# Which 39 of 128 expert blocks are computed ahead of the expert loop and stored

## The chip, the cores and the metric

The kernel runs on one core of a Trainium2 chip. The metric is the device time of one execution in microseconds (us), the median of several runs. Before the change it is 2943.44 us (three runs, 2942.09 to 2951.27).

Five engines matter. PE is the matrix engine (PEld are its weight loads), DVE the vector engine, ACT the activation engine, POOL issues the indirect gathers, and SP issues the plain DMAs. Each works through its own instructions in a fixed order and waits on semaphores for the others.

## The reference

One decoder layer over 1024 tokens of width 1024, all in float32. A mixing part (retention heads and differential attention heads, an output projection and a residual) comes first. Then follows a layer of product-key experts:

```python
q = (xb @ wq).reshape(t, PEER_HEADS, 2, PEER_DQ // 2)
s = jnp.einsum('thpd,hpkd->thpk', q, subkeys).astype(jnp.float32)
s_top, i_top = lax.top_k(s, K)
cand = (s_top[:, :, 0, :, None] + s_top[:, :, 1, None, :]).reshape(t, PEER_HEADS, K * K)
c_top, c_idx = lax.top_k(cand, K)
...
e = i1 * N_KEYS + i2
g = jax.nn.softmax(c_top, axis=-1)
ue = jnp.take(u, e, axis=0)
ve = jnp.take(v, e, axis=0)
act = jax.nn.gelu(jnp.einsum('thkd,td->thk', ue, xb).astype(jnp.float32), approximate=False)
return jnp.einsum('thk,thkd->td', (g * act).astype(xb.dtype), ve)
```

There are 8 heads, 16 ranks in each (`K`) and 128 x 128 = 16384 experts. Each expert is one row of `u` and one of `v`. A residual and a final norm follow.

## The kernel before

**Two ways through the experts.** Tokens lie in eight tiles of 128. Five of them (640 tokens, `TB`) are "dense": every expert is computed for all of them, and a weight matrix that is zero nearly everywhere (`g_d` in DRAM) selects. The other three are "sparse": for each of them 128 rows of `u` and 128 rows of `v` are gathered by indirect DMA (POOL, L860 and L867), 768 gathers of 512 KB in all, and each is worked into the result by one DVE instruction (L862 for `u`, L869 for `v`). Five buffers (`ug`) hold gathered rows.

**The dense experts.** The 16384 experts are 128 blocks of 128. For one block, `experts_in` (L711) loads a block of `u` (`uraw`, L704, 512 KB), splits it into a high part (ACT, L706) and a low part (DVE, L708), runs 48 matmuls into two PSUM banks `psH` (L720 to L722: two halves of 320 tokens, eight chunks, three products each) and writes the GELU of it (ACT, L723) into a tile `ga` of 128 x 640. `ga` has two buffers, which all the blocks use in turn.

**Stored blocks.** Some blocks are computed before the expert loop, in `spills` (L728), woven between the steps of the routing and of `dense_routes`, and their activations are stored in DRAM (`hs_d`, 320 KB each). There are `SPILL` = 39 of them, those of the list `early`.

**The expert loop.** It runs over 32 groups of `EG` = 4 blocks. One group does this:

- One DMA loads the group's weights from `g_d` into `gt` (L787, 1280 KB, in runs of 512 bytes). `gt` has a single buffer, so the load waits until the last use of the group before.
- For each of its four blocks: the activations come either from `experts_in`, or, for a block in `early`, by one DMA from `hs_d` into a tile of the same two buffers (L802, called `gl` in the profile). DVE multiplies them in place by the weights (L806), ACT and DVE split the product into high and low parts `wh` (L810) and `wl` (L812). The block of `v` (`vraw`, L814, 512 KB) is loaded and split likewise (`vh` L816, `vl` L818).
- Then 120 matmuls of 512 columns (L794 to L796): ten units (five tiles, two halves) by four blocks by three products. Four units stay in PSUM over the whole loop (`kp`), six go through two PSUM banks `psV` and are added into SBUF by DVE after each group (L830, called room, acc, accS, accc_intra and accab).

**What sets the order.** A planner orders each engine's instructions at build time: it runs the program on a model of the engines, and whenever an engine is free in the model it takes the instruction that is ready and stands earliest in the program text. The text has the dense loop first and the gathers after it, so the gathers fill the places that the dense work leaves free in the model. On the chip this order is fixed: an instruction that has to wait holds up everything behind it on its engine. Gathers can start before the loop at a pace set by hand (`PER`); from the first L806 on they are free.

Of the kernel before, what the change touches and what calls it, by code (L numbers as in the profile page):

```python
# [27 lines left out]
DC = D // P  # L28
# [4 lines left out]
NK = 128  # L33
# [13 lines left out]
EG = 4  # L47
# [3 lines left out]
KL = 1  # L51
BIGS = 4
ROUTE = 6
MIX = 3
ACTS = 1
AHEAD = 1
SPILL = 39
# [42 lines left out]
def layer_kernel(ctx, tc, x, wt, wn, wo, wq, sk, ut, u, v, gmix, gffn, gfin, gsub, dlam, consts, alb, out):  # L100
    nc = tc.nc
    V, A, PE, G, SY = nc.vector, nc.scalar, nc.tensor, nc.gpsimd, nc.sync
# [16 lines left out]
    one = cp.tile([P, 1, 1], U32, name="one")  # L119
# [11 lines left out]
        return r  # L131

    def front(m, pp, cst, g0, nt, dense, late):
        """Steps of the layer up to the routing for tiles g0..g0+nt, in the rooms m."""
        n = nt * P
        first, last = g0 == 0, g0 + nt == NT
        halves = [(0, n)] if n <= 512 else [(0, n // 2), (n // 2, n)]
# [8 lines left out]
            return m.big[0].tile(shape, dt, tag=m.big[1], bufs=m.big[2], name=name)  # L146

        def chunk(src, shape):
            """Weights [128, k, m] in their hi and lo parts."""
            raw = wp.tile(shape, F32, tag="raw", bufs=RAW, name="wraw")  # L150
            SY.dma_start(raw, src)
            hi = wp.tile(shape, F32R, tag="uh", bufs=2, name="whi")
            A.activation(hi, raw, AF.Copy)  # L153
            lo = wp.tile(shape, F32R, tag="ul", bufs=2, name="wlo")
            V.tensor_sub(lo, raw, hi.bitcast(F32))  # L155
            return hi, lo

        def mm(ps, a, b, start, stop):
            """Adds the product of operands a and b, each (hi, lo)."""
            PE.matmul(ps, a[0], b[0], start=start, stop=False)  # L160
            PE.matmul(ps, a[0], b[1], start=False, stop=False)  # L161
            PE.matmul(ps, a[1], b[0], start=False, stop=stop)
# [33 lines left out]
            yield  # L196

        def split_t(src_of, name):
            """Transposes natural [128 t, 1024] tiles into [128, DC, n] operands."""
            th = m.hp.tile([P, DC, n], F32R, tag="hTh", name=name + "h")  # L200
            tl = m.hp.tile([P, DC, n], F32R, tag="hTl", name=name + "l")
            for t in range(nt):
                src = src_of(t)
                srcs = src if isinstance(src, tuple) else (src[:, :512], src[:, 512:])
                for q in range(2):
                    ps = bankB("psX").rearrange("p (c t) -> p c t", c=4)
                    for c in range(4):
                        PE.transpose(ps[:, c], srcs[q][:, c * P:(c + 1) * P], ident)
                    dst = th[:, 4 * q:4 * q + 4, t * P:(t + 1) * P]
                    A.activation(dst, ps, AF.Copy)  # L210
                    V.tensor_sub(tl[:, 4 * q:4 * q + 4, t * P:(t + 1) * P], ps, dst.bitcast(F32))
                yield "turned"
            return th, tl

        # input norm
        gm = big([P, D], "gmix")
        SY.dma_start(gm, gmix.to_broadcast([P, D]))

# [10 lines left out]

        yield "normed"  # L230

        # natural projections: rv, dv, rg
        rv = m.vp.tile([P, nt, 512], F32, tag="rv", name="rv")

        def put_dv(t, ps):
# [160 lines left out]
                V.scalar_tensor_tensor(yd[:, t, sl], yd[:, t, sl], rd[:, t, h:h + 1], cst["gsub"],  # L396
                                       op0=ALU.mult, op1=ALU.mult)

        # output projection and residual
        mx = yield from split_t(lambda t: (rg[:, t], yd[:, t]), "m")  # L400
        x2 = [p.tile([P, nt, 512], F32, tag=tg, name="x2" + tg) for p, tg in ((m.vp, "rv"), (fp, "R"))]
        for hf in range(2):
# [68 lines left out]
            yield  # L471

    class Routed:
        """What the routing of a group leaves for later: key ranks and scores."""

        def __init__(self, rp, nt, tags):
            n = nt * PH * K
# [3 lines left out]
            self.ci = rp.tile([P, nt, PH, K], U32, tag=tags[1], name="late1")  # L481

    def decode(rp, late, t, eqs=("eq", 1), tmp=("tmp", 1), cs=("c2", 1)):
        """Key indices i1, i2 of tile t as [token, (head, rank)]."""

        tmps = rp.tile([P, 7, PH, K], U32, tag=tmp[0], bufs=tmp[1], name="tmps")
        row, col, sh, up = (tmps[:, i] for i in range(4))
        shf = tmps[:, 4].bitcast(F32)
        V.tensor_single_scalar(row, late.ci[:, t], 4, op=ALU.logical_shift_right)
        V.tensor_single_scalar(col, late.ci[:, t], K - 1, op=ALU.bitwise_and)  # L490
        V.tensor_scalar(shf, row, 1.0, -1.0, op0=ALU.max, op1=ALU.mult)
        V.tensor_scalar_add(sh, shf, 5.0)
        V.tensor_tensor(up, col, sh, op=ALU.logical_shift_right)
        V.tensor_tensor(row, one.to_broadcast([P, PH, K]), row, op=ALU.logical_shift_left)
        V.tensor_single_scalar(row, row, 1, op=ALU.logical_shift_right)
        c2 = rp.tile([P, 2, PH * K, 2], F16, tag=cs[0], bufs=cs[1], name="c2")

        def two(a):
            return a.rearrange("p h k -> p (h k)")[:, :, None].to_broadcast([P, PH * K, 2])
        V.tensor_tensor(c2[:, 0], two(row), two(up), op=ALU.add)  # L500
        V.tensor_tensor(up, up, sh, op=ALU.logical_shift_left)
        V.tensor_tensor(c2[:, 1], two(col), two(up), op=ALU.subtract)
        ij = []
        for p in range(2):
            eq = rp.tile([P, PH, K, K], F16, tag=eqs[0], bufs=eqs[1], name="eq")
            V.tensor_tensor(eq.rearrange("p h k (a b) -> p (h k) a b", b=2),
                            iok.rearrange("p (a b) -> p a b", b=2)[:, None].to_broadcast([P, PH * K, K // 2, 2]),
                            c2[:, p, :, None].to_broadcast([P, PH * K, K // 2, 2]), op=ALU.is_equal)
            V.tensor_tensor(eq, eq, late.tf[:, t, :, p, None, :].to_broadcast([P, PH, K, K]), op=ALU.mult)
            w = K // 2  # L510
            while w > 1:
                V.tensor_add(eq[:, :, :, :w], eq[:, :, :, :w], eq[:, :, :, w:2 * w])
                w //= 2
            iF = tmps[:, 5 + p].bitcast(F32)
            V.tensor_add(iF, eq[:, :, :, 0], eq[:, :, :, 1])
            ij.append(iF)
        return ij

    def gates_of(rp, late, nt, tag):
        """Softmax of the scores of tiles 0..nt, in their place."""  # L520
        cv = late.cv.rearrange("p t h k -> p (t h) k")
        mz = rp.tile([P, 2, nt * PH], F32, tag=tag[0], bufs=tag[1], name="mz")
        V.tensor_copy(mz[:, 0], cv[:, :, 0])
        V.tensor_sub(cv, cv, mz[:, 0, :, None].to_broadcast([P, nt * PH, K]))
        A.activation(cv, cv, AF.Exp)
        V.tensor_reduce(mz[:, 1], cv, axis=AX.X, op=ALU.add)
        V.reciprocal(mz[:, 1], mz[:, 1])
        V.tensor_mul(cv, cv, mz[:, 1, :, None].to_broadcast([P, nt * PH, K]))

    def sparse_routes(rp, late, g0, nt, *rooms):  # L530
        """Steps that leave expert indices and weights of the sparse tiles."""
        gates_of(rp, late, nt, rooms[0])
        for lt in range(nt):
            t = ST.index(g0 + lt)
            V.tensor_copy(gA[t].rearrange("p (h k) -> p h k", h=PH), late.cv[:, lt])
            i1, i2 = decode(rp, late, lt, *rooms)
            V.scalar_tensor_tensor(i1, i1, float(NK), i2, op0=ALU.mult, op1=ALU.add)
            V.tensor_copy(idxA[t].rearrange("p (h k) -> p h k", h=PH), i1)
            yield

    def dense_routes(rp, gp, pp, late):
        """Steps that put the weight matrices of the dense tiles into DRAM."""
        before = None
        gates_of(rp, late, ND, ("mz", 1))
        for t in range(ND):
# [17 lines left out]
        yield from build_g(gp, pp, *before)  # L563

    def build_g(gp, pp, r, lo, tb):
        """Weight matrices of one token tile: G[i2, i1, token] into DRAM."""
        for s in range(P // GC):
            st = gp.tile([P, NK, GC], F32, tag="st", bufs=2, name="st")
            for q in range(GC // 8):
# [78 lines left out]
        return es.enter_context(tc.tile_pool(name=name, bufs=1, reuse_waits="tile", **kw))  # L648

    def weave(a, b, na=1, nb=1):  # L650
        """Steps of a and b in turn, nb of b to na of a."""
        i = j = 0
        while a is not None or b is not None:
            if b is None or (a is not None and i * nb <= j * na):
                i += 1
                try:
                    yield next(a)
                except StopIteration:
                    a = None
            else:  # L660
                j += 1
                try:
                    yield next(b)
                except StopIteration:
                    b = None
# [5 lines left out]
        return next(i for i in reversed(ins) if i.engine == V.engine).name  # L671

    def gated(g, per):
        """Opens the way for per of the gathered experts after each step of g."""
        due = 0.0
        for y in g:
            due += per[y == "turned"]
            while due >= 1.0:
                gates.append(last_dve())
                due -= 1.0  # L680
            yield y
# [27 lines left out]
        return uh, ul  # L709

    def experts_in(ei, bank):  # L711
        """Activations of 128 experts for all dense tokens: [expert, token]."""
        uh, ul = load_u(ei)
        xh, xl = late.nx
        ga = wp.tile([P, TB], F32, tag="ga", bufs=2, name="ga")
# [7 lines left out]
            A.activation(ga[:, sl], ps, AF.Gelu)  # L723
        return ga

    early = [ei for ei in range(NK) if ei % EG < MIX][:SPILL]

    def spills(pf):  # L728
        for i, ei in enumerate(early):
# [46 lines left out]
        V.scalar_tensor_tensor(j, acc, r, gfb, op0=ALU.mult, op1=ALU.mult)  # L776
        SY.dma_start(out[t], j)

    # experts of the dense tiles
    acc = {}  # L780
    for i, un in enumerate(units[KEEP:]):
        acc[un] = room[i]
# [56 lines left out]
                V.tensor_copy(a[:, sl], acc[t, hf])  # L839
        finish(dp, a, DT[t], wp.tile([P, D], F32, tag="raw", bufs=RAW, name="fin"))  # L840

    # experts of the sparse tiles, gathered
    nth = 0

    def gate(ins):
# [63 lines left out]
```

## Time and profile before

| | |
|---|---|
| median of the runs | 2943.44 us |
| span of the profiled execution | 2961.6 us |
| PE busy | 2799.5 us, 95% |
| DVE busy | 2355.3 us, 80% |
| ACT busy | 1064.6 us, 36% |
| POOL busy | 1056.9 us, 36% |
| moved by DMA | 742.90 MB, mean 251 GB/s |

The profile is of one execution, whose span was 18.2 us (0.6%) over the median of the timed runs. The expert loop takes from about 1370 us to the end; the mixing and the routing lie before it. The busy share of PE is an average over stages with different limits, and its matmuls overlap in time, so that the step from one matmul's start to the next one's, not the duration, says how fast they run.

### The profile page before, as it was taken

The numbers are of one execution on the slowest core, as the hardware profiler recorded it, in microseconds if no ns is written. First come the engines' busy times: TensorE is split into PE (matmuls) and PEld (weight loads), VectorE is DVE, ScalarE is ACT, GpSimd is POOL, SyncE is SP. The second block draws the span as 40 slices with busy tenths as digits, with TensorE's granted clock in tenths as the row PEclk, the third lists the DMA queues.
The fourth block names the chain that finished last, engine by engine and source line by source line (L and its number), as shares of the span: only waits on it lengthen the run. The fifth ranks groups of instructions, "written<-read, shape, count | busy, mean of one in ns | idle before, by whom it ended". The sixth has DMA issues, their size and how long they took to land.

```text
span 2961.6 us, 43054 instructions
## 1 busy us (share of the span) xinstructions
PE 2799.5 (95%) x16043; PEld 2478.4 (84%) x16043; DVE 2355.3 (80%) x4522; ACT 1064.6 (36%) x1882; POOL 1056.9 (36%) x786
## 2 busy tenths in 40 slices
PE   7989989998889999999989999999999999999998
PEld 6868877776679999998777788899989989999987
DVE  3455888756769999985777888888889988888988
ACT  4553334433333248996212222222322222222222
POOL 0000003423330000001545444566566666665554
PEclk9989998876989999999999999999999999999999
DMA  5334236744662226667888888899999999999997
GB/s 166 108 121 140 94 118 206 247 150 152 241 239 89 85 97 226 242 240 285 305 293 305 308 301 312 318 330 334 344 337 336 341 341 335 341 338 321 344 339 264
DMA packets 293956, 742.90 MB, mean 251 GB/s; under 512 B 23529, under 2 KB 118761, under 8 KB 293746
## 3 DMA queue, kind: packets, MB, share of 16 engines
q0 software_dynamic: 112320, 405.06, 38.8%
q1 hardware_dynamic: 181426, 335.09, 33.0%
q8 instruction: 125, 2.05, 0.3%
q14 instruction: 85, 0.70, 0.1%
HBM read 670.92 MB, written 69.14 MB: 250 GB/s over the span
## 4 chain that ended last, share of the span: by engine, by line
PE 35%; issue 27%; DMA 11%; DVE 9%; POOL 4%; ACT 1%; POOLq 0%; DVEq 0%; ACTq 0%
DMA gt<-g_d 5%; PE psH L722 4%; PE psH L721 4%; PE psH L720 4%; POOL vg L867 3%; DMA vg<-in_v,idx 3%; PE psV L794 3%; PE psV L795 3%; PE psV L796 3%; DMA gl<-hs_d 2%; DVE sa L869 2%; PE kp L795 2%; PE kp L794 2%; PE kp L796 2%; DVE vl L818 1%
## 5 line engine op out<-in xcount | busy, mean ns | idle before, releaser
L867 POOL DMA_INDIRECT vg<-in_v,idx x384 | 528.5, 1376 | 923.0 <-DVE ug L862 521.5
L860 POOL DMA_INDIRECT ug<-in_u,idx x384 | 520.9, 1356 | 522.1 <-DVE ug L862 370.7
L869 DVE SCALAR_TENSOR_TENSOR sa<-vg,shs,sa 128x1024 f32<-128x1024 f32 x384 | 492.4, 1282 | 42.3 <-DMA vg<-in_v,idx 38.7
L862 DVE SCALAR_TENSOR_TENSOR ug<-ug,sx 128x1024 f32<-128x1024 f32 x384 | 461.2, 1222 | 62.6 <-DMA ug<-in_u,idx 61.9
L720 PE MATMUL psH<-nh,uh 128*128 128x320 f32 x1424 | 439.7, 309 | 0.1
L721 PE MATMUL psH<-nl,uh 128*128 128x320 f32 x1424 | 439.6, 309 | 0.0
L722 PE MATMUL psH<-nh,ul 128*128 128x320 f32 x1424 | 438.7, 309 | 0.8 <-DVE ul L708 0.8
L794 PE MATMUL psV<-vh,wh 128*128 128x512 f32 x768 | 306.8, 401 | 36.3 <-DVE acc L830 35.8
L795 PE MATMUL psV<-vl,wh 128*128 128x512 f32 x768 | 305.0, 398 | 0.0
L796 PE MATMUL psV<-vh,wl 128*128 128x512 f32 x768 | 297.4, 396 | 0.0
L720 PEld LDWEIGHTS psH<-nh,uh 128*128 128x128 f32 x1424 | 267.5, 188 | 6.4 <-ACT uh L706 0.9
L721 PEld LDWEIGHTS psH<-nl,uh 128*128 128x128 f32 x1424 | 267.3, 188 | 5.2
L722 PEld LDWEIGHTS psH<-nh,ul 128*128 128x128 f32 x1424 | 267.1, 188 | 4.4 <-DVE ul L708 1.6
L723 ACT ACTIVATE ga<-psH 128x320 f32<-128x320 f32 x178 | 74.6, 426 | 438.4 <-PE psH L722 396.4
L706 ACT ACTIVATE uh<-uraw 128x1024 fp32r<-128x1024 f32 x128 | 135.7, 1060 | 209.7 <-PE psH L721 120.3
L794 PEld LDWEIGHTS psV<-vh,wh 128*128 128x128 f32 x768 | 147.9, 193 | 68.7 <-DVE acc L830 38.6
L720 PE MATMUL psHs<-nh,uh 128*128 128x320 f32 x624 | 196.3, 316 | 9.1 <-ACT ga L723 8.9
L153 ACT ACTIVATE whi<-wraw 128x1024 fp32r<-128x1024 f32 x104 | 110.1, 1059 | 258.4 <-PE psT L161 141.4
L155 DVE TENSOR_TENSOR wlo<-wraw,whi 128x1024 fp32r<-128x1024 f32 x104 | 126.9, 1220 | 94.6 <-ACT whi L153 92.3
L795 PE MATMUL kp<-vl,wh 128*128 128x512 f32 x512 | 199.2, 392 | 0.4 <-DVE vl L818 0.4
L794 PE MATMUL kp<-vh,wh 128*128 128x512 f32 x512 | 193.2, 393 | 4.7 <-ACT wh L810 4.7
L708 DVE TENSOR_TENSOR ul<-uraw,uh 128x1024 fp32r<-128x1024 f32 x128 | 156.4, 1222 | 48.7 <-ACT uh L706 48.6
(242 smaller groups left out, 6271.0 us busy)
## 6 DMA issues: line engine op xcount, KB each, us to landing
uraw<-in_ut SPq DMA_DIRECT2D x128, 512.0 KB, 6.3
vraw<-in_v SPq DMA_DIRECT2D x128, 512.0 KB, 6.9
g_d<-st SPq DMA_DIRECT2D x80, 512.0 KB, 4.7
gt<-g_d SPq DMA_DIRECT2D x32, 1280.0 KB, 18.0
wraw<-in_wt SPq DMA_DIRECT2D x32, 512.0 KB, 3.7
wraw<-in_wq SPq DMA_DIRECT2D x32, 512.0 KB, 3.8
hs_d<-ga SPq DMA_DIRECT2D x39, 320.0 KB, 2.6
gl<-hs_d SPq DMA_DIRECT2D x39, 320.0 KB, 5.9
```

Of the source, the lines that this page charges most:

```text
L706: A.activation(uh, raw, AF.Copy)
L708: V.tensor_sub(ul, raw, uh.bitcast(F32))
L720: PE.matmul(ps, uh[:, dc], xh[:, dc, sl], start=(dc == 0), stop=False)
L721: PE.matmul(ps, uh[:, dc], xl[:, dc, sl], start=False, stop=False)
L722: PE.matmul(ps, ul[:, dc], xh[:, dc, sl], start=False, stop=(dc == DC - 1))
L794: PE.matmul(ps, Wh[e][:, sl], Vh[e][:, so], start=start, stop=False)
L795: PE.matmul(ps, Wh[e][:, sl], Vl[e][:, so], start=False, stop=False)
L796: PE.matmul(ps, Wl[e][:, sl], Vh[e][:, so], start=False, stop=stop)
L860: G.indirect_dma_start(out=ug, out_offset=None, in_=u, in_offset=bass.IndirectOffsetOnAxis(ap=idxA[t][:, k:k + 1], axis=0))
L862: gate(V.scalar_tensor_tensor(ug, ug, 1.0, xt, op0=ALU.mult, op1=ALU.mult, accum_out=hs[:, k:k + 1]))
L867: G.indirect_dma_start(out=vg, out_offset=None, in_=v, in_offset=bass.IndirectOffsetOnAxis(ap=idxA[t][:, k:k + 1], axis=0))
L869: gate(V.scalar_tensor_tensor(ac, vg, hs[:, k:k + 1], ac, op0=ALU.mult, op1=ALU.add))
```

## The change

The list of stored blocks changes. Before, with `MIX` = 3, it held the first three of each group of four for groups 0 to 12. Now it holds the first block of all 32 groups and, with `MIX` = 4, the second block of every fourth group (0, 4, ... 24). It is 39 blocks in both.

```diff
-MIX = 3
+MIX = 4
...
-    early = [ei for ei in range(NK) if ei % EG < MIX][:SPILL]
+    shared = list(range(0, NK, EG))
+    early = shared + [g * EG + 1 for g in range(0, NK // EG, MIX)][:SPILL - len(shared)]
```

So groups 0 to 12 computed one block in the loop and loaded three, and groups 13 to 31 computed four. Now 25 groups compute three and load one, and seven groups compute two and load two. The rest of the diff takes comments out.

## Rows read from the trace of the kernel before

**Rows 1.** Stretches: us, busy of each engine (instructions), PE clock, DMA share, GB/s.

```profile
1408.66:1838.34 429.68, 394.00 (x1847) 334.29 (x1846) 342.63 (x372) 96.04 (x126) 201.53 (x144) 0.96 0.88 302
1931.45:2874.20 942.75, 942.23 (x5300) 860.11 (x5299) 828.88 (x1004) 242.32 (x347) 587.29 (x424) 1.00 0.95 337
```

**Rows 2.** SP's timeline: gt loads that bound the two stretches (start, us).

```profile
1408.66 0.37 SPq L787 DMA_DIRECT2D gt<-g_d  x1
...
1838.38 0.38 SPq L787 DMA_DIRECT2D gt<-g_d  x1
...
1931.48 0.38 SPq L787 DMA_DIRECT2D gt<-g_d  x1
...
2874.25 0.38 SPq L787 DMA_DIRECT2D gt<-g_d  x1
```

**Rows 3.** PE's timeline near 2248 and 2264 us: starts of matmuls.

```profile
2248.02 0.31 PE L721 MATMUL psH<-nl,uh 128*128 128x320 f32 x1
...
2248.90 0.31 PE L721 MATMUL psH<-nl,uh 128*128 128x320 f32 x1
...
2264.15 0.39 PE L794 MATMUL psV<-vh,wh 128*128 128x512 f32 x1
...
2268.00 0.39 PE L796 MATMUL kp<-vh,wl 128*128 128x512 f32 x1
```

**Rows 4.** Waits of PE in the first stretch: total us, times, longest.

```profile
PE psV L794 <- DVE acc L830: 34.7, 9, 5.6
```

**Rows 5.** Waits of DVE in the first stretch.

```profile
DVE gl L806 <- DMA gt<-g_d: 56.3, 9, 9.9
DVE gl L806 <- DMA gl<-hs_d: 14.3, 4, 7.2
```

**Rows 6.** DVE's timeline in one group of the first stretch.

```profile
1607.63 0.82 DVE L806 TENSOR_TENSOR ga<-ga,gt 128x640 f32<-128x640 f32 x1
...
1616.33 1.29 DVE L830 TENSOR_TENSOR room<-psV,room 128x512 f32<-128x512 f32 x2 [1.06 <-PE psV L796]
1617.53 1.27 DVE L869 SCALAR_TENSOR_TENSOR sa<-vg,shs,sa 128x1024 f32<-128x1024 f32 x1
1625.03 0.83 DVE L806 TENSOR_TENSOR gl<-gl,gt 128x640 f32<-128x640 f32 x1 [6.22 <-DMA gt<-g_d]
...
1628.43 0.69 DVE L830 TENSOR_TENSOR acc<-psV,acc 128x512 f32<-128x512 f32 x1
```

**Rows 7.** PE's timeline in the same group.

```profile
1629.17 0.50 PE L794 MATMUL psV<-vh,wh 128*128 128x512 f32 x1 [1.47 <-DVE acc L830]
```

**Rows 8.** Issues of the gt load, first stretch, then second: count, KB each, us to landing.

```profile
gt<-g_d SPq DMA_DIRECT2D x11, 1280.0 KB, 17.5
...
gt<-g_d SPq DMA_DIRECT2D x17, 1280.0 KB, 19.0
```

**Rows 9.** DVE's timeline in one group of the second stretch.

```profile
2261.93 0.82 DVE L806 TENSOR_TENSOR ga<-ga,gt 128x640 f32<-128x640 f32 x1
...
2294.08 0.81 DVE L806 TENSOR_TENSOR ga<-ga,gt 128x640 f32<-128x640 f32 x1
```

**Rows 10.** The gt load over the first stretch: its landing, least, median and most.

```profile
DMA to landing us min/median/max: 13.6/17.7/19.1
```

**Rows 11.** POOL's timeline near the end: two gathers that follow each other.

```profile
2701.98 1.28 POOL L867 DMA_INDIRECT vg<-in_v,idx  x1 [0.65 <-DVE sa L869]
2703.91 1.86 POOL L867 DMA_INDIRECT vg<-in_v,idx  x1 [0.65 <-DVE sa L869]
```

**Rows 12.** DVE's gather work by line, first stretch, then second.

```profile
L869 DVE SCALAR_TENSOR_TENSOR sa<-vg,shs,sa 128x1024 f32<-128x1024 f32 x125 | 160.3, 1282 | 6.0 <-DMA vg<-in_v,idx 4.9
L862 DVE SCALAR_TENSOR_TENSOR ug<-ug,sx 128x1024 f32<-128x1024 f32 x18 | 21.8, 1223 | 0.0
...
L869 DVE SCALAR_TENSOR_TENSOR sa<-vg,shs,sa 128x1024 f32<-128x1024 f32 x221 | 283.4, 1282 | 31.7 <-DMA vg<-in_v,idx 29.6
L862 DVE SCALAR_TENSOR_TENSOR ug<-ug,sx 128x1024 f32<-128x1024 f32 x202 | 242.6, 1223 | 35.9 <-DMA ug<-in_u,idx 35.7
```

## The prediction, made before the changed kernel was run

> **What bounds the kernel now.** I read the page's slices first. PE is busy everywhere, but DMA and DVE are lower around 1400 to 1850 us than after it. That is the expert loop's first part, the 13 groups that compute one block and load three. So I read the loop in two stretches, cut at starts of the gt load, which comes once in a group.
>
> First stretch: from 1408.66 to 1838.38 us there are eleven groups of one computed block [rows 2], 39.07 us each. PE's clock was at 0.96 of full speed, DMA at 0.88 [rows 1]. Second stretch: from 1931.48 to 2874.25 us there are 17 groups of four computed blocks [rows 2], 55.46 us each. PE was busy for 942.23 of 942.75 us, at full clock [rows 1].
>
> What would PE need alone? Six steps of psH take from 2248.02 to 2248.90, 0.147 us each; 17 steps of 512-column matmuls take from 2264.15 to 2268.00, 0.2265 us each [rows 3]. A computed block has 48 of the first, 7.0 us, and a group has 120 of the second, 27.2 us. That makes 34.2, 41.3, 48.3 and 55.3 us for one to four computed blocks. The last agrees with the 55.46 measured: the second stretch is bound by PE. The groups of the first lose 39.07 - 34.2 = 4.9 us each.
>
> The waits say how. PE waited nine times, 34.7 us in all, to start an output matmul (psV) until DVE had added up the bank of PSUM before it [rows 4]. DVE had not done that because the instruction ahead of it in its order, the first multiplication by the weights of the next group (L806), waited for that group's gt or its stored block: 56.3 + 14.3 = 70.6 us [rows 5]. One group shows the chain. The last L806 of a group ends at 1608.45 and frees the single gt buffer; DVE does its next instructions up to 1618.80, waits 6.22 us for the load, multiplies at 1625.03, and adds at 1628.43 [rows 6]; PE, which stood 1.47 us for it, goes on at 1629.17 [rows 7]. So the load takes 17.5 us [rows 8], and DVE has put the multiplication behind some 10 us of work: the order was planned for a shorter load.
>
> In the second stretch nothing of the kind happens. The first block of a group is computed there, its activations come late, and its multiplication stands at 2294.08, 31.3 us after the last one of the group before (2262.75) [rows 9], where the load of 19.0 us [rows 8] has long landed.
>
> **The change part by part.** 39 blocks are computed ahead as before, in as many steps, so the time up to the loop costs nothing either way; only the addresses differ. In the loop the sums are the same too: 13 x 1 + 19 x 4 = 89 computed blocks before, 25 x 3 + 7 x 2 = 89 after. What moves are 26 blocks each way. A computed block in a group means a load of 512 KB on SP, a conversion each on ACT and DVE, 48 matmuls and two GELUs; a stored one means a load of 320 KB on SP. SP's order and the shared ga buffers move with them: a stored load waits until a buffer is free, with the vraw and uraw loads behind it.
>
> (a) Gain on PE. If PE sets the pace of every group, the loop takes 25 x 48.3 + 7 x 41.3 = 1497 us, against 13 x 39.07 + 19 x 55.46 = 1562 now: 65 us less. It is the most that the change can bring.
>
> (b) Cost on DVE. Every group now begins with a stored block. Its multiplication needs nothing but gt, as in the first stretch, so the planner can set it again as soon as its model has the load landed, ahead of the psV sums. The stall that 13 groups had then comes to 32. DVE's busy time was 342.63 / 11 = 31.1 us in a group of one computed block and 828.88 / 17 = 48.8 in one of four [rows 1]; in between, 5.9 us a block, I put 37.0 for two and 42.9 for three. The gathers are in it: (125 + 18) / 11 = 13.0 and (221 + 202) / 17 = 24.9 a group [rows 12], so 17.0 and 20.9; in a straight line their sum over the loop stays what it was.
>
> The stall is the size that decides. Its bounds are zero, as in the second stretch, and the longest one seen, 9.9 us [rows 5]. The mean of the first stretch is 70.6 / 11 = 6.4. The load takes longer with more traffic, 17.5 us at 302 GB/s and 19.0 at 337 [rows 1, 8]; the new groups, at about 316 GB/s (5.3 MB of loads and 21 gathers of 0.52 MB in 51 us), add 0.6. I take 7.0. DVE's other idle time in the first stretch is (429.7 - 342.6 - 70.6) / 11 = 1.5 us.
>
> A group of three then takes DVE 42.9 + 7.0 + 1.5 = 51.4 us and one of two 45.5, more than PE's 48.3 and 41.3. The same sum for one computed block gives 31.1 + 6.4 + 1.5 = 39.0, what was measured, so in a group with this stall DVE, not PE, has set the time. The loop takes 25 x 51.4 + 7 x 45.5 = 1604 us, 42 us more. What goes: the 4.9 us that PE lost in each of 13 groups; what is late next: PE loses 3.1 us in each of 25 and 4.2 in each of seven. Each microsecond of stall is worth 32 us. At 5.7 the change is worth nothing, and under 3.9 PE takes over in the groups of three.
>
> (c) The tail. PE and the gathers end together now; with gathers spread in a straight line nothing changes there. ACT is busy for 242.32 of 942.75 us where four blocks are computed [rows 1], so its two conversions hide in any group.
>
> The sum is +42 us on the profiled execution (span 2961.6, 18.2 over the median); on the median of 2943.4 it gives 2985 us.
>
> One rule of the Trainium skill speaks against this. The gt load takes 13.6 us at the least in the first stretch [rows 10]. The page "DMA: Bandwidth & Descriptors", section "Anatomy of one DMA", fits 2.0 us and the bytes over 436 GB/s for one transfer: 5.0 us for this load, an estimate, which DVE would never wait for. The trace does not agree: 17.5 to 19.0, with gathers on the same engines. By the page the sum would be that of (a) alone.
>
> **Rivals.**
>
> *No stall: the load hides.* The multiplication stands later in DVE's order, or the matmuls of two or three computed blocks give PE enough to do while DVE waits. For it: four-block groups have it at 31.3 us, and the planner has twice or three times as many psH matmuls to put before the waiting psV. Against it: those matmuls stand in a fixed order too, planned for a load that is early. The time is 2943 - 65 = 2878.
>
> *Half a stall.* DVE reaches the multiplication later, since it also waits for gathers in a denser order; at a stall of 4.5 us a group of three takes 48.9, one of two 43.0, the loop 1524: -38, 2905. For it: loads as short as 13.6 us [rows 10]. Against it: longer loads with more traffic.
>
> *Gathers left for the end, on top of the stall.* If the planner finds room for one gather less in a group than the straight line says, 32 remain after the loop. There they go at the pace of POOL, 2703.91 - 2701.98 = 1.93 us each [rows 11], while the loop saves 1.28 us of DVE for each [rows 12]: 32 x 0.65 = 21 us more, 3006. Two less make 3027. It decides from the first gather that starts after the last psV sum. For it: the stored multiplication comes earlier in every group and leaves DVE less open time. Against it: DVE's open time in the plan depends on blocks, whose sum stays.
>
> **How the numbers follow.** The forecast, a stall of about 7 us in every group, gets 0.53; no stall 0.22; half a stall 0.13; gathers left over 0.12. A measurement of this kernel can tell about 0.3%, 9 us, from no change. The forecast's own range goes with stalls from 5.7 to 8.5 us, 2943 to 3033; some 0.06 of its chance lies within 9 us. Half a stall gives 0.10 to faster and 0.03 to no change, leftover gathers 0.10 to slower and 0.01 to each of the others. That makes faster 0.22 + 0.10 + 0.01 = 0.33, same 0.06 + 0.03 + 0.01 = 0.10, slower 0.47 + 0.10 = 0.57. The range of 8 in 10 goes from 2882, which leaves half of the no-stall case out, to 3035.
>
> **What would show it.** In the profile after, DVE's waits at the first L806 of a group: some 200 us in all for gt and stored blocks over 32 groups, where 11 groups had 70.6. Groups of 51 us between gt loads, with PE waiting for DVE's sum in most of them. The forecast is wrong if gt loads come 48.3 us apart and PE waits nowhere, or if the first L806 of a group stands 20 us or more after the last of the group before without a wait; a string of gathers after the last psV sum would speak for the third rival.

## The result and the profile after

The changed kernel takes 3054.63 us (median of four runs, 3053.14 to 3074.22) against 2943.28 beside it: 111 us slower, a ratio of 1.0385 with an interval of 1.0353 to 1.0417. The forecast had the direction and the stall of DVE in every group, but not what the stall costs: it had 42 us, and 3054.63 lies above its range. The profiled execution had a span of 3052.6 us, 91.0 more than that of before.

The loop in stretches, with the columns of [rows 1]. The first goes from the second to the last gt load, 30 groups; the other is the end:

```profile
1412.80:2963.20 1550.40, 1456.66 (x7614) 1292.64 (x7613) 1244.23 (x1486) 361.82 (x504) 807.52 (x598) 0.97 0.86 307
2963.20:3052.60 89.40, 71.56 (x358) 61.87 (x356) 73.74 (x83) 20.18 (x34) 40.07 (x31) 0.92 0.75 258
```

Before, the same 30 groups took 2874.25 - 1408.66 = 1465.6 us [rows 2], so 84.8 of the 91 us are here. The end took nearly as long as before, 89.4 us against 87.3. PE's clock is at 0.97 over all of these 30 groups, where before it was at 0.96 in the first stretch alone [rows 1].

What PE and what DVE waited for in this stretch (total us, times, longest), PE first, then DVE:

```profile
PE psV L795 <- DVE acc L831: 87.4, 27, 5.5
```

```profile
DVE gl L807 <- DMA gt<-g_d: 160.9, 25, 8.5
...
DVE gl L807 <- DMA gl<-hs_d: 36.8, 5, 8.9
```

These answer to [rows 4] and [rows 5]. DVE's wait is 197.7 us over 30 groups, 6.6 each, where 11 groups had 6.4 each. PE waits 2.9 us a group for the sum behind it, where it had 34.7 / 11 = 3.2. So the wait has come to every group, as big as it was. The gt load lands after 17.7 us at the median here. The Trainium skill ("DMA: Bandwidth & Descriptors", "Anatomy of one DMA") fits its 2.0 us and bytes over 436 GB/s to DMAs issued from gpsimd. This load is issued by SP, and the estimate of 5.0 us that the forecast made with that fit is as far off as before.

One group, with three computed blocks, on DVE; its gt load was issued at 2491.90:

```profile
2491.06 0.82 DVE L807 TENSOR_TENSOR ga<-ga,gt 128x640 f32<-128x640 f32 x1
...
2499.77 1.28 DVE L831 TENSOR_TENSOR room<-psV,room 128x512 f32<-128x512 f32 x2
2509.31 0.83 DVE L807 TENSOR_TENSOR gl<-gl,gt 128x640 f32<-128x640 f32 x1 [8.26 <-DMA gt<-g_d]
...
2511.93 0.68 DVE L831 TENSOR_TENSOR acc<-psV,acc 128x512 f32<-128x512 f32 x1
```

It is [rows 6] again: after the last multiplication of a group DVE is at its other instructions for 9.2 us (up to 2501.05), then stands before the first one of the next. PE at the same time:

```profile
2507.18 0.39 PE L796 MATMUL psV<-vl,wh 128*128 128x512 f32 x1
2507.41 0.39 PE L797 MATMUL psV<-vh,wl 128*128 128x512 f32 x1
...
2509.83 0.31 PE L721 MATMUL psH<-nl,uh 128*128 128x320 f32 x1
2512.67 0.79 PE L795 MATMUL psV<-vh,wh 128*128 128x512 f32 x1 [2.53 <-DVE acc L831]
...
2514.12 0.63 PE L795 MATMUL psV<-vh,wh 128*128 128x512 f32 x1
2514.54 0.63 PE L796 MATMUL psV<-vl,wh 128*128 128x512 f32 x1
```

PE has psH matmuls of the next group to do, but only as many as its fixed order has there; then it stands 2.53 us. After the wait the step between output matmuls is 0.42 us instead of 0.23: PE goes on at half its clock. The stretches of that moment (columns of [rows 1]; the clock is the third number from the end):

```profile
2492.00:2503.00 11.00, 11.00 (x59) 9.71 (x58) 7.62 (x13) 1.08 (x2) 6.08 (x5) 1.00 1.02 346
2503.00:2512.00 9.00, 7.14 (x38) 6.04 (x36) 2.69 (x5) 0.74 (x1) 0.45 (x1) 1.00 0.50 184
2512.00:2516.00 4.00, 3.33 (x8) 2.65 (x9) 4.00 (x8) 0.00 (x0) 2.51 (x2) 0.51 0.39 131
2516.00:2520.00 4.00, 4.00 (x16) 3.42 (x15) 4.00 (x8) 0.55 (x1) 3.31 (x3) 0.64 0.78 243
```

So this one short stall has two costs on PE: the time it stands, and the time after it at 1.2 instead of 2.4 GHz.

### The profile page after: what moved, and what is told of

Read it like the earlier page. It is cut to its first block, busy times and chain, and to the rows that moved or that the text cites. A ratio compares the mean times of both kernels' runs of the same rounds, so it can differ in the third digit from the quotient of the medians.

```text
span 3052.6 us, 43044 instructions
## 1 busy us (share of the span) xinstructions
PE 2826.2 (93%) x16043; PEld 2497.6 (82%) x16043; DVE 2354.3 (77%) x4522; ACT 1065.7 (35%) x1882; POOL 1033.6 (34%) x786
## 4 chain that ended last, share of the span: by engine, by line
issue 23%; PE 18%; DMA 16%; DVE 15%; POOL 11%; ACT 3%; POOLq 0%; SPq 0%; DVEq 0%; ACTq 0%
POOL vg L868 6%; DMA vg<-in_v,idx 5%; POOL ug L861 5%; DMA gt<-g_d 4%; DMA ug<-in_u,idx 3%; DVE ug L863 3%; DVE sa L870 2%; PE psHs L720 2%; PE psHs L722 2%; PE psHs L721 2%; PE psG L592 2%; DMA vraw<-in_v 1%; ACT st L594 1%; PE psT L160 1%; PE psT L161 1%
## 5 line engine op out<-in xcount | busy, mean ns | idle before, releaser
L868 POOL DMA_INDIRECT vg<-in_v,idx x384 | 508.8, 1325 | 981.7 <-DVE ug L863 524.3
L795 PE MATMUL psV<-vh,wh 128*128 128x512 f32 x768 | 320.6, 417 | 94.3 <-DVE acc L831 90.9
L796 PE MATMUL psV<-vl,wh 128*128 128x512 f32 x768 | 316.5, 412 | 0.0
L797 PE MATMUL psV<-vh,wl 128*128 128x512 f32 x768 | 309.9, 409 | 0.0
L811 ACT ACTIVATE wh<-gl 128x640 fp32r<-128x640 f32 x39 | 28.8, 739 | 526.7 <-DVE gl L807 493.9
L817 ACT ACTIVATE vh<-vraw 128x1024 fp32r<-128x1024 f32 x128 | 127.9, 1051 | 231.5 <-PE psV L797 122.5
## 6 DMA issues: line engine op xcount, KB each, us to landing
gt<-g_d SPq DMA_DIRECT2D x32, 1280.0 KB, 17.7
```

The source lines that it names most:

```text
L795: PE.matmul(ps, Wh[e][:, sl], Vh[e][:, so], start=start, stop=False)
L796: PE.matmul(ps, Wh[e][:, sl], Vl[e][:, so], start=False, stop=False)
L797: PE.matmul(ps, Wl[e][:, sl], Vh[e][:, so], start=False, stop=stop)
L817: A.activation(vh, vr, AF.Copy)
L868: G.indirect_dma_start(out=vg, out_offset=None, in_=v, in_offset=bass.IndirectOffsetOnAxis(ap=idxA[t][:, k:k + 1], axis=0))
```

## The experiments

Theory A: a multiplication that is ready as soon as gt is there gets a place in DVE's order that is too early for the real load, and that wait alone, with the slow clock after it, is the 91 us. The rivals: B, spreading itself costs (traffic, gathers, DVE's load in every group); C, the wait only moves, since a single gt buffer holds the group anyway; D, DVE's busy time and waits set the pace and PE only follows, as the forecast had it.

**The sums first (e1).** An ordering is added to the changed kernel, without a wait on the chip: the first multiplication of a group comes behind a given sum in DVE's order.

```diff
-            V.tensor_mul(gv, gv, gt[:, :, e])
+            ins = V.tensor_mul(gv, gv, gt[:, :, e])
+            if g and e == 0:
+                tc.add_manual_dep(ins.ins, sums[3], ...)   # the fourth psV sum of the group before
...
+        sums = []
...
                 V.tensor_add(acc[un], ps, acc[un])
+                sums.append(last_dve())
```

> The changed kernel with one ordering added: the first multiplication of a group's weights stands behind the fourth psV sum (accS) of the group before in DVE's order. Theory A (the multiplication of a stored first block is set before the load of its weights has landed, and that wait alone costs the time): DVE's wait for gt and the stored block falls from some 200 us to under 50, PE waits under 1 us a group, its clock stays at 1.0, gt loads come 48 us apart in groups of three computed blocks, and the time is 2870 to 2910 us. Theory B (spreading itself costs: denser gathers, more traffic or DVE's load in every group, the place of the multiplication is a symptom): 3020 us or more. Theory C (the wait only moves: DVE waits as long at the later place): 3040 to 3060.

Measured: 2945.13 us, a ratio to the kernel before of 0.9977 (0.9953 to 1.0001). One ordering takes back all that the change cost. The loop's 30 groups take 1451.5 us, 99 less than in the changed kernel. But the forecast of this run was 2870 to 2910: waits of DVE remain at multiplications, 72.0 us, on stored blocks above all:

```profile
DVE gl L807 <- DMA gl<-hs_d: 51.5, 9, 8.2
...
DVE ga L807 <- DMA gt<-g_d: 13.7, 3, 6.7
DVE gl L807 <- DMA gt<-g_d: 6.8, 4, 2.2
```

**The same in the kernel before (e2).**

> The kernel before with the same ordering. Theory A: the 13 groups of one computed block lose their wait and come to PE's 34.2 us from 39.1; 2875 to 2895 us, level with the changed kernel with this ordering, since what is left is PE's time, which is the same in both. Theory B: 2935 to 2950, as it is. Theory C: the loop of load and multiplications (17.5 us and 21 us) holds these groups at 39 us: 2940.

Measured: 2948.57 us, 0.9995 (0.9972 to 1.0018): nothing gained, where theory A gave 2875 to 2895; as in theory C. DVE's timeline in one of the first groups shows another reason:

```profile
1526.16 0.83 DVE L806 TENSOR_TENSOR gl<-gl,gt 128x640 f32<-128x640 f32 x1 [8.48 <-DMA gl<-hs_d]
1526.90 1.28 DVE L875 SCALAR_TENSOR_TENSOR sa<-vg,shs,sa 128x1024 f32<-128x1024 f32 x1
1528.10 0.68 DVE L835 TENSOR_TENSOR acc<-psV,acc 128x512 f32<-128x512 f32 x1
...
1529.89 0.68 DVE L835 TENSOR_TENSOR accS<-psV,accS 128x512 f32<-128x512 f32 x1
1530.50 0.81 DVE L806 TENSOR_TENSOR gl<-gl,gt 128x640 f32<-128x640 f32 x1
```

A multiplication still stands ahead of acc and waits. It cannot be the one of the first stored block, which comes behind accS; it is that of the second, which was not ordered. The run did not test what it was meant to; e9 does.

**A buffer of its own for the first block's weights (e3).** The order is left to the planner; what makes the multiplication wait is taken away.

```diff
-        gt = lp.tile([P, NGC, EG, GC], F32, tag="rv", name="gt")
+        g0t = dp.tile([P, NGC, GC], F32, tag="gt0", name="gt0")
+        SY.dma_start(g0t, g_d[:, :, g * EG * GC:(g * EG + 1) * GC].rearrange("c p x -> p c x"))
+        gt = lp.tile([P, NGC, EG - 1, GC], F32, tag="rv", name="gt")
...
-            V.tensor_mul(gv, gv, gt[:, :, e])
+            V.tensor_mul(gv, gv, gt[:, :, e - 1] if e else g0t)
```

> The changed kernel with the first block's weights in a tile and a load of their own, which can start as soon as the first multiplication of the group before is done; the order is left to the planner. The two loads move the same bytes in runs of 128 and 384 instead of 512. Theory A: no wait at the first multiplication, and one at the second in the seven groups with two stored blocks; 2880 to 2920 us, more where the shorter runs slow the loads. Theory B: 3020 or more.

Measured: 3038.06 us, 1.0281 (1.0252 to 1.031), far from what theory A gave. The stretches, from the second to the last load of the main part, and the end:

```profile
1416.60:2825.00 1408.40, 1408.40 (x7624) 1264.49 (x7623) 1154.73 (x1411) 365.09 (x504) 734.50 (x525) 1.00 0.93 310
2825.00:3040.50 215.50, 70.91 (x364) 61.91 (x362) 171.56 (x159) 20.18 (x34) 136.47 (x107) 0.68 0.85 292
```

PE stands nowhere in 30 groups, its clock is full, and they take 1408.4 us; PE's own time by the forecast is 24 x 48.3 + 6 x 41.3 = 1407. So in the loop the wait was worth up to 1550.4 - 1408.4 = 142 us (it also holds fewer gathers than the changed kernel's, 525 of POOL's instructions against 598; e10 below takes 1410.2 with 602). The end is 126 us longer. DVE's gather work in that end (count, busy, mean, idle before):

```profile
L872 DVE SCALAR_TENSOR_TENSOR sa<-vg,shs,sa 128x1024 f32<-128x1024 f32 x111 | 142.5, 1283 | 28.5 <-DMA vg<-in_v,idx 26.5
```

It is 111 instructions; the changed kernel has 35 such from its last gt load on. That is what the forecast's third rival described: the planner gave the gathers fewer places in the loop. Why it did so with this edit is not shown. Theory A was right on the loop here and wrong on the sum, since the planner makes the order anew for each edit.

**The last block stored (e4).**

```diff
-    shared = list(range(0, NK, EG))
-    early = shared + [g * EG + 1 for g in range(0, NK // EG, MIX)][:SPILL - len(shared)]
+    shared = list(range(3, NK, EG))
+    early = shared + [g * EG + 2 for g in range(0, NK // EG, MIX)][:SPILL - len(shared)]
```

> The changed kernel with the last block of each group stored instead of the first, and the third one too in every fourth group. In DVE's order the first multiplication, now of a computed block, still stands within some 11 instructions of the last one of the group before in about half of the groups, and some 25 behind it in the others. Theory A: a wait in that half, none in the others; 2940 to 2990 us. A rival by which it matters that a stored block comes first: 2870 to 2900. Theory B: 3020 or more.

Measured: 2935.59 us, 0.994 (0.9919 to 0.9961), 4 us under the range of theory A, and 0.6% faster than the kernel before. DVE's waits at multiplications:

```profile
DVE ga L807 <- DMA gt<-g_d: 70.5, 15, 7.3
...
DVE gl L807 <- DMA gl<-hs_d: 16.0, 11, 3.7
```

15 waits in 30 groups are for gt, with the multiplication of a computed block. That a stored block stands first is not needed: it is enough that the first block's activations are ready early.

**Both together (e5), and one sum later (e6, with `sums[4]`).**

> The last block of each group stored, and the first multiplication of a group behind the fourth psV sum of the group before. DVE's order now has 13 or more instructions between the last multiplication of a group and the first of the next in nearly all groups. Theory A, additive (each wait of PE and the half-speed clock after it are added to PE's own time of 48.3 and 41.3 us a group): waits at the first multiplication fall to under 50 us over the loop, and the time is 2895 to 2925 us, faster than the kernel before. Theory D (DVE's busy time and its waits set the pace, PE only follows): DVE's work is the same, so no less than the 2935 of the run with the last block stored alone.

> As the run with the last block stored and the first multiplication behind the fourth sum, but behind the fifth. Theory A: the later place takes what is left of the wait, 2890 to 2920 us, level or faster. Rival: the later multiplication makes the output matmuls of the next group wait for their operands and gives the gain back, 2930 or more.

Measured: 2907.21 us, 0.9853 (0.9814 to 0.9891), and 2909.71, 0.9859 (0.9815 to 0.9903); both beat both kernels, the kernel before by some 1.4%, and the place one sum later makes no difference that the intervals can tell. The loop of e5:

```profile
1398.29:2815.21 1416.92, 1406.62 (x7588) 1259.20 (x7587) 1248.86 (x1488) 363.11 (x503) 811.65 (x601) 1.00 0.95 337
```

DVE is busy for 1248.86 us in it, in the changed kernel for 1244.23. The same work of DVE fits into 133 us less. So DVE's busy time alone did not set the pace, which is how the expectation of e5 words theory D. The forecast's own sum counts DVE's waits too, and e5 does not test it: the waits at multiplications fell from 197.7 us to 21.9, and with so few of them that sum also leaves the pace to PE. e1 and e4 lie between. Reckoned from their traces, with the waits put into the forecast's sum group by group, it gives 1437 and 1429 us for the 30 groups; PE's own 1407 with PE's waits (29.8 and 28.0) and its slower clock gives 1449 and 1442; 1451.5 and 1445.2 were measured. The changed kernel parts the two sums more widely (below).

**The changed kernel and the kernel before once more (e7, e8).**

> The changed kernel once more, to see how much of the time lies before the loop: the first gt load started at 1368 us in its first profile and at 1370 in that of the kernel before, but at 1354 in the two runs with the sums first. If this is chance of one execution, it may come at 1354 here and the span at about 3040; if the change moves it, 1368 again. The loop between the second and the last gt load is 1550 us in both theories, within 10.

> The kernel before once more, for the same question: its first profile had a span of 2961.6 with the first gt load at 1370 us, where the timed runs had a median of 2943. If the stretch before the loop varies from one execution to the next, a load at 1354 us and a span of 2945; the loop between the second and the last gt load 1462 to 1468 us.

Measured: spans of 3043.0 and 2960.3 us; from the second to the last gt load 1552.4 and 1465.1 us, both within some 2 us of the first time. The first gt load came at 1359.5 and 1367.8 us, 8.5 and 2.4 earlier than the first time. So the loops repeat. The stretch before them varied in the changed kernel; the kernel before came nearly as late again, and the 1354 and 2945 of its expectation did not appear.

**All multiplications behind the fourth sum.** The condition of e1 becomes `if g:`, in the kernel before (e9), with the last block stored (e10) and in the changed kernel (e11).

> The kernel before with all multiplications of a group, not only the first, behind the fourth psV sum of the group before. In the run that ordered the first alone, the one of the second stored block took its place and waited instead. Theory A: the 13 groups come from 39.1 us to within 1.5 of PE's 34.2, and the time falls by 40 to 60 us against the kernel before (2890 to 2912 where that has 2951), level with the spread kernels: then spreading was no part of the gain. Theory C (a single gt buffer holds a group of one computed block at its load of 17.5 us and some 21 us of multiplications, in whatever order): no change, 2940 to 2955.

> The last block of each group stored and all multiplications behind the fourth sum. Nearly the same order as with the first one alone, which had 10.8 us of gaps on PE in the loop: 2900 to 2915 us in theory A, which leaves only the few groups in which the second stood early.

> The changed kernel (first block stored) with all multiplications behind the fourth sum. Theory A: the waits of the seven groups with two stored blocks go, some 15 us less than with the first alone; 2920 to 2935 us. If the place of the stored block in the group matters beyond this wait, it stays over 2935 while the kernel with the last block stored has some 2907.

Measured: 2911.69 us, 0.9879 (0.9863 to 0.9896); 2901.55, 0.9854 (0.9819 to 0.9889); 2908.63, 0.9872 (0.984 to 0.9903). The first two lie in the ranges of theory A, e11 11 us under its range. Theory C falls: the groups of one computed block come from 39.1 to 35.7 us ((1785.72 - 1393.33) / 11, at their gt loads), 1.5 over PE's 34.2. Below are eleven groups of e9, which answer to the first row of [rows 1], and then the 30 groups of e11, which answer to those of the changed kernel above:

```profile
1393.33:1785.72 392.39, 384.12 (x1850) 326.03 (x1849) 347.57 (x378) 97.11 (x126) 220.96 (x147) 0.99 0.95 334
```

```profile
1398.05:2822.44 1424.39, 1412.46 (x7609) 1265.63 (x7609) 1241.15 (x1483) 361.47 (x504) 827.49 (x597) 1.00 0.94 333
```

The changed list and the old one, each with its multiplications in place, differ by nothing that these intervals can tell. Theory B falls: spreading the stored blocks costs nothing that they can tell, and it brings nothing either. All of the 111 us hangs on where the multiplications stand, with the order that the planner makes around them: it sets everything anew, so no run moves the multiplications alone. The work in the loop stays the same (DVE is busy for 1241.15 us in e11 and 1244.23 in the changed kernel, with 597 and 598 of POOL's gathers).

## Why the prediction was wrong

- *What bounds the kernel, and how the first groups lose 4.9 us:* right. e9 takes 3.4 of it away, in the very groups in which it was read.
- *(a), the most to gain is PE's own time:* right as a bound. e3 runs the 30 groups at it, within 1.5 us.
- *(b), the stall comes to all groups:* right. Forecast 7.0 us a group and some 200 in all, measured 6.6 and 197.7 (in 30 groups), so the rival of half a stall is out. DVE's busy time was forecast at 24 x 42.9 + 6 x 37.0 = 1252 us and measured at 1244.
- *(b), what the stall costs:* here it failed. The step is "A group of three then takes DVE 42.9 + 7.0 + 1.5 = 51.4 us and one of two 45.5, more than PE's 48.3 and 41.3", and the conclusion that DVE had set the time. It compares two sums and takes the larger, so that PE's own loss is counted only as far as DVE's sum exceeds PE's time. The size of the stall was not at fault: with 6.6 in place of 7.0 the same step gives 24 x 51.0 + 6 x 45.1 = 1495 us for the 30 groups that took 1550. PE stays the bound and loses its 4.9 us in a group of any size: the wait of some 3 us for the bank and the slower clock after it. Adding the 4.9 gives 53.2 and 46.2 us; measured between gt loads are 53.1 (24 groups) and 46.1 (six), a loss of 4.8 in both, where the forecast had 3.1 and 4.2. The loop comes to 25 x 53.2 + 7 x 46.2 = 1653, 92 us over the 1562 of before; the spans differ by 91.0. That DVE's sum gave 39.0 for the first stretch was no proof: PE's 34.2 with 3.2 of wait [rows 4] and 0.04 x 39.1 = 1.6 of clock [rows 1] gives 39.0 as well. Told as a sum of DVE, the term that was too small is its other idle time: put at 1.5 us a group, it was 10.2 - 6.6 = 3.6 in the changed kernel, 2.4 of it before gather work (43.9 and 28.9 us in all). The one account does not exclude the other, but PE's, with its measured waits and clock, comes within 4 us of the loop in e1, e4 and the changed kernel.
- *The same for the whole stretch:* PE waited 87.4 + 3.4 us for DVE's sums and 2.9 for ACT; a mean clock of 0.97 costs about 0.03 x 1550 = 47. With PE's 1407 that makes 1548, and 1550.4 were measured.
- *(c), the tail, and the third rival:* the tail stayed, as forecast; leftover gathers came only in e3.
- *No stall:* this rival needed the multiplication later in DVE's order. It was not in the changed kernel; put there (e11), it gives 2909, not 2878, with PE's waits down to 12 us and the 30 groups still 17 over PE's 1407.
- *From the profile to the runs:* the profiles explain 91 of 111 us, all of it from the first gt load on. The profiled execution of before was 18 us over its median, as the forecast said. The runs of the kernel before that stand beside e1 to e4 go from 2938.92 us, at a mean clock of 0.967, to 2969.28, at 0.957. In the 13 profiles of this study the first gt load came anywhere from 1353 to 1372 us, with the kernel before at 1370.2 and 1367.8. The clock between 500 and 850 us was lower where it came late; first the kernel before, then e5, where it came at 1353.9:

```profile
500.00:850.00 350.00, 325.95 (x1472) 250.13 (x1472) 233.65 (x430) 127.74 (x310) 129.84 (x110) 0.80 0.63 210
```

```profile
500.00:850.00 350.00, 310.11 (x1528) 239.79 (x1528) 252.44 (x465) 138.77 (x339) 139.42 (x116) 0.89 0.66 222
```

  That this spread is what parts the 20 us between runs and profile fits, but no run shows it; it stays open.

## What to carry to other kernels

When a wait comes to groups that are bound by another engine, add what that engine lost per wait, standing and slow clock together, to its own time; do not set the two engines' sums side by side and take the larger. In a kernel whose order is fixed by a model, look for the instruction that gets a place before its load has landed on the chip: all that stands behind it on its engine is late with it. (That the planner's model has the gt load land too early is read from the order; no run shows the model itself.) An ordering that adds no wait of its own, here the multiplications behind the sums, was worth more than the distributions of the work that were tried without it: 2901.55 to 2911.69 us with it (e5, e6, e9 to e11), against 2935.59 with the last block stored, 3054.63 with the first, and 2948 to 2951 for the kernel before beside the ordered ones. It has to cover every multiplication that can be ready early: with the first alone (e1, e2) the times stayed at 2945 and 2949.

## What the runs showed of the hardware that was not expected

- A wait of PE of 2.5 us was followed by a granted clock of 0.51 over the next 4 us and 0.64 over the 4 after them, so that the waits cost about half as much again (in the changed kernel's 30 groups 94 us of waits and about 47 of clock). Not every wait was followed by it: after 21 of the 32 waits of PE over 0.3 us in these groups the granted clock was at its lower level for a time, after the other 11 it stayed full.
- Loads in runs of 128 and 384 bytes instead of 512 (e3) did not slow the loop: PE waited for nothing in 1408.4 us, at a DMA share of 0.93. But issuing the load in runs of 128 held SP for 2.5 us at the median and up to 10.3 (the other load 0.38 at the median).
